# A hybrid decoder step: the down projection product by product over all of K, with the residual kept in SBUF

## The chip, the cores and the metric

The kernel runs on one core of one Trainium2 chip. The metric is the device time of one execution in microseconds. The kernel before took 2302.09 us (median of 3 runs, 2299.87 to 2306.37). One further execution was recorded by the hardware profiler; all profile lines of the kernel before come from it.

## The reference

One inference step of a decoder with a single layer, on 1040 prompt tokens (16 learned meta tokens and 1024 prompt tokens) and 8 sample tokens, 1048 tokens in all, in float32. The layer is a half-step feed-forward network (FFN), a mixer (HGRN2 heads and Mamba-2 heads) and a second half-step FFN:

```python
h = h + 0.5 * swiglu(rmsnorm(h, n1), w1g, w1u, w1d)
u = rmsnorm(h, nm) @ w_in            # then the HGRN2 and Mamba-2 groups
h = h + concat(hgrn_out, ssm_out) @ w_out
h = h + 0.5 * swiglu(rmsnorm(h, n2), w2g, w2u, w2d)
y = rmsnorm(h, norm_final)

def swiglu(x, wg, wu, wd):
    return (silu(x @ wg) * (x @ wu)) @ wd   # 1024 -> 2816 -> 1024
```

The change touches the last product of each `swiglu`, `(...) @ wd`, with the residual addition `h + 0.5 * (...)`, and what follows directly on it: the norm that feeds the mixer, and the final norm.

## The kernel before

**Layout.** Activations lie transposed: channels on the 128 partitions, the 1048 tokens along the free dimension. Tokens are cut into quarters of Q = 262; a half `c` has two quarters.

**Precision.** `Core.split` makes of a float32 tensor a rounded part (a cast on ScalarE, L137) and a remainder (a subtraction on VectorE, L138). `mm3` then issues three matmuls, high x high, high x low and low x high (L143 to L145).

**Seven products.** Each matrix product is done with one level of Strassen's scheme: a 2 x 2 block product with seven block products, numbered 1 to 7, in the Winograd form. The left operands are sums of weight blocks, the right operands sums of activation blocks. In the FFN a product's right operand has 262 columns for each of two halves.

**Gate/up phase.** `pair` does one block of 128 hidden channels of gate and up: 7 products x 2 halves x 4 blocks of K x 3 matmuls. There are 22 pairs, and each two of them make one hidden pair `i` (0 to 10). `left` loads four weight blocks (L320), forms four sums (L325) and seven splits; `Hidden.jobs` forms the seven right operands of the down phase for that hidden pair (subtractions at L503), splits each and stores the split halves to DRAM (tiles `hd`, L510).

**Down phase.** `down` takes the hidden pairs in three groups of 3, 4 and 4 (`Hidden.GROUPS`). For each group, and in it for each of four pairs of output tiles `j`, it runs all seven products and adds the partial result to the residual. So `Hidden.load` reads the split operands of a whole group at the group's start (L532, 28 transfers), `load_h` and `store_h` read and write the residual tiles for each group (L552, L559), and `left` reads the weights of a (group, j) once and forms all seven left operands. The posts (L570 to L580) combine the PSUM results: product 1 goes to a temporary on ScalarE (L573), 6 adds to it (L575), 2 closes the common part (L579, L580), the others are added with L570.

**Order.** Within the FFN the order on TensorE, VectorE, ScalarE and SP is written out by hand. A `Steps` object holds one step for each (product, half); other work is hung in front of a step by number (`S.before`), so a lead of 10 means ten steps ahead. Every engine works through its own queue in that order. All FFN transfers are issued by SP, one behind the other; an issue that waits holds all behind it.

**Buffers.** Tiles of 1056 columns come in 30 "u" slots and 8 "s" slots; weight buffers are 6 split (`ws`) and 8 raw (`r`); PSUM has two pairs of banks (`acc`) and four single banks (`mis`).

**Behind the phase.** `after1` squares and sums the residual for the next norm (`Norm.add`, ScalarE L201 and POOL L202), finishes the norm (`Norm.end`, a matmul with ones at L209), and forms the mixer's input (`plain_x`, L225 to L228). `after3` runs nine `final` blocks of 128 tokens each: transposes (L1365), squares (L1366), the scaling (L1372) and the store of the output.

Of the kernel before, what the change touches and what calls it, by code (L numbers as in the profile page):

```python
# [181 lines left out]
class Norm:  # L182
# [10 lines left out]
    def add(self, k, q):  # L193
        K = self.K
        hs = self.h[k][:, q * Q : q * Q + Q]
        if k == 0:
            self.sq[q] = K.t(Q)
            self.an = K.nc.scalar.activation(self.sq[q], hs, AF.Square)
        else:
            t = K.t(Q)  # L200
            self.an = K.nc.scalar.activation(t, hs, AF.Square)  # L201
            K.nc.gpsimd.tensor_add(self.sq[q], self.sq[q], t)  # L202

    def end(self, q, table=True):
        K = self.K
        if q % 2 == 0:
# [104 lines left out]
def left(K, S, s0, srcs, n, at, spare=None):  # L311

# [14 lines left out]
    def split(i, p):  # L327
        w[p] = K.split_w(raw[p], spare() if spare and i == 6 else None)
# [8 lines left out]
    splits = [lambda i=i, p=p: split(i, p) for i, p in enumerate(ORDER)]  # L337
# [11 lines left out]
def product(K, ps, w, op, n, first, last):  # L349
    for k in range(n):  # L350
        ks = slice(k * Q, k * Q + Q)
        wh, wl = (w[:, o + k * P : o + k * P + P] for o in (0, 512))
        K.mm3(ps, wh, wl, op[0][:, ks], op[1][:, ks], first and k == 0, last and k == n - 1, not first)


class Unit:
# [17 lines left out]
    def step(self, S, p, c, cs, mis=False):  # L374
        def mm():
            new = p in (1, 6, 5, 7)
            b = self.bank(p, cs, mis)
            product(self.K, b[:, cs.index(c)], self.w[p], self.ops[c][p], self.n, new, True)
# [87 lines left out]

class Hidden:

    GROUPS = (3, 4, 4)

    def __init__(self, K):
        self.K = K
        self.d = {}
        for g, n in enumerate(self.GROUPS):
            for p in ORDER:
                self.d[g, p] = K.dram.tile([P, 4, n, Q], F32, name=K.uid("hd"))
        self.of = [(g, i) for g, n in enumerate(self.GROUPS) for i in range(n)]
        self.n = 0  # L480

    def jobs(self, S, i, hid, e0, e1):

        K = self.K
        nc = K.nc
        g, j = self.of[i]
        t, b = {}, {}
        last = i == len(self.of) - 1
# [8 lines left out]
        def sub(p, x, y):  # L497
# [5 lines left out]
            nc.vector.tensor_sub(b[p], val(x), val(y))  # L503

        def split(p, w):
            self.n += 1
            st = K.slot("s" if last or self.n % 5 in (0, 2, 4) else "u", T, F32R)
            hi, lo = st[:, : 2 * Q], st[:, 2 * Q :]
            K.split(val(p), hi, lo)
            S.before(w, lambda: nc.sync.dma_start(self.d[g, p][:, :, j, :], st.bitcast(F32).rearrange("p (a t) -> p a t", a=4)))  # L510

        def at(i, fn, *args):
            S.before(i, lambda: fn(*args))

        at(e0 + 1, sub, 5, 12, 1)
        for k, p in ((3, 1), (5, 5)):
            at(e0 + k, split, p, e0 + k + 2)
        ks = range(1, 9) if last else range(1, 17, 2)
        for k, (fn, *args) in zip(ks, ((sub, 6, 3, 5), (split, 2), (sub, 7, 3, 12), (split, 3), (split, 6), (sub, 4, 2, 6), (split, 7), (split, 4))):
            at(e1 + k, fn, *args, *((e1 + k + 2,) if fn is split else ()))  # L520

    def load(self, S, g, s0, lead, tags):

        K = self.K
        n = self.GROUPS[g]
        ops = [{}, {}]

        def get(p, c, tag):
            ops[c][p] = []
            for part in range(2):  # L530
                t = K.slot(tag, n * Q, F32R)
                K.nc.sync.dma_start(t.bitcast(F32), self.d[g, p][:, 2 * part + c].rearrange("p n t -> p (n t)"))  # L532
                ops[c][p].append(t)

        for i, (p, c) in enumerate((p, c) for p in ORDER for c in range(2)):
            S.before(s0 + i - min(lead, 13 + i if tags[i] == "u" else 99), lambda p=p, c=c, i=i: get(p, c, tags[i]))
        return ops


def down(K, S, wdv, n, f0, j, ops, src, dst=None, h=None, then=None):  # L540

# [1021 lines left out]
```

## Time and profile before

| | |
|---|---|
| median of 3 runs | 2302.09 us |
| lowest, highest | 2299.87, 2306.37 us |
| the profiled execution | 2297.2 us |
| its span, first to last instruction | 2295.5 us |
| mean granted TensorE clock | 0.952 |
| busy: TensorE, VectorE, ScalarE, POOL | 2040.8, 1456.7, 799.2, 137.1 us |
| bytes moved by DMA | 353.11 MB |

How to read the lines that follow. PE is TensorE, PEld its weight loads, DVE VectorE, ACT ScalarE, SP the engine that issues the transfers. In a row of slices each digit is a fortieth of the span (57.4 us) and gives a busy share in tenths; PEclk is the clock granted to TensorE in tenths of full speed. A row of stretches gives, for each engine, the busy time and the number of instructions, and then the granted clock, the DMA engines' busy share and what they moved in GB/s (a share can slightly exceed 1). A wait row gives who waited for what, in total us, how many times, and the longest. A timeline row gives start and duration in us, engine, source line, operation and shape, and in brackets the idle time before it and what ended it. A row of one source line gives durations in ns (least, median, greatest), then first and last start in us.

### The profile page before, as it was taken

How to read it: one execution, taken by the hardware profiler on the slowest of the kernel's cores; microseconds unless marked ns; L12 is line 12 of the kernel's file. 1: busy time of each engine (PE TensorE's matmuls, PEld its weight loads, DVE VectorE, ACT ScalarE, POOL GpSimd, SP SyncE). 2: the span in 40 equal slices, each digit the busy share in tenths (PEclk: the TensorE clock that was granted, in tenths of full speed). 3: DMA queues.
4: the chain of work that ended last, by engine and by line, in shares of the span. 5: the costliest groups of instructions: out<-in, count | busy, mean ns of one | idle time of the engine just before them, and what ended most of it. 6: DMA issues, size and time to landing. Idle time of an engine off the chain costs nothing.

```text
span 2295.5 us, 38684 instructions
## 1 busy us (share of the span) xinstructions
PE 2040.8 (89%) x15550; PEld 1982.3 (86%) x15550; DVE 1456.7 (63%) x2516; ACT 799.2 (35%) x1511; POOL 137.1 (6%) x175
## 2 busy tenths in 40 slices
PE   3899999997787979979999999969999999778796
PEld 3799999997787869868989988869999999778795
DVE  5677777765454666577455456876777767554465
ACT  5433333332111353463432344433333333212122
POOL 1000000000000210131011101200000000000000
PEclk8999999998899989989999999989999999889897
DMA  3445445469869421163022153214454545986931
GB/s 114 122 131 160 140 132 158 136 183 322 316 242 345 143 82 35 60 178 87 30 66 75 34 170 124 90 38 131 144 151 136 162 128 167 352 288 233 353 122 75
DMA packets 344315, 353.11 MB, mean 154 GB/s; under 512 B 19584, under 2 KB 301440, under 8 KB 344128
## 3 DMA queue, kind: packets, MB, share of 16 engines
q1 hardware_dynamic: 343320, 348.49, 46.8%
q8 instruction: 123, 2.02, 0.4%
q10 hardware_dynamic: 592, 2.10, 0.3%
q14 instruction: 56, 0.46, 0.1%
q0 software_dynamic: 224, 0.04, 0.0%
HBM read 226.68 MB, written 123.95 MB: 153 GB/s over the span
## 4 chain that ended last, share of the span: by engine, by line
PE 45%; DVE 5%; DMA 4%; ACT 1%; issue 1%; SPq 0%; POOL 0%; DVEq 0%; ACTq 0%; POOLq 0%
PE acc L143 14%; PE acc L144 13%; PE acc L145 13%; DMA r<-in_w_ffn_down_dram 2%; PE mis L1234 2%; DMA u<-hd 1%; DVE r L325 0%; DVE u L1372 0%; PE mis L1273 0%; DVE s L1351 0%; DVE u L138 0%; DVE ws L138 0%; DVE u L253 0%; PE mis L1291 0%; PE mis L1329 0%
## 5 line engine op out<-in xcount | busy, mean ns | idle before, releaser
L143 PE MATMUL acc<-u,ws 128*128 128x262 f32 (+2 forms) x4512 | 1335.8, 297 | 162.1 <-ACT ws L137 74.2
L144 PE MATMUL acc<-u,ws 128*128 128x262 f32 (+2 forms) x4512 | 1324.6, 294 | 13.8 <-DVE u L138 10.7
L145 PE MATMUL acc<-u,ws 128*128 128x262 f32 (+2 forms) x4512 | 1322.1, 294 | 0.0
L143 PEld LDWEIGHTS acc<-u,ws 128*128 128x128 f32 x4512 | 866.1, 192 | 182.9 <-ACT ws L137 78.7
L144 PEld LDWEIGHTS acc<-u,ws 128*128 128x128 f32 x4512 | 870.9, 193 | 16.3 <-DVE u L138 12.2
L145 PEld LDWEIGHTS acc<-u,ws 128*128 128x128 f32 x4512 | 866.2, 192 | 0.4
L138 DVE TENSOR_TENSOR ws<-r,ws 128x512 fp32r<-128x512 f32 (+1 forms) x562 | 380.2, 680 | 252.7 <-ACT ws L137 251.7
L137 ACT CAST ws<-r 128x512 fp32r<-128x512 f32 (+1 forms) x562 | 325.4, 606 | 337.2 <-DMA r<-in_w_ffn_down_dram 126.7
L325 DVE TENSOR_TENSOR r<-r,r 128x512 f32<-128x512 f32 (+1 forms) x272 | 181.1, 679 | 126.8 <-DMA r<-in_w_ffn_down_dram 108.1
L421 ACT ACTIVATE t<-t 128x524 f32<-128x524 f32 (+1 forms) x46 | 28.7, 623 | 320.9 <-DVE t L420 320.9
L570 DVE SCALAR_TENSOR_TENSOR s<-acc,s 128x524 f32<-128x524 f32 (+1 forms) x120 | 78.6, 655 | 87.0 <-PE acc L145 86.1
L202 POOL TENSOR_TENSOR t<-t,t 128x262 f32<-128x262 f32 x56 | 48.5, 877 | 889.6 <-ACT t L201 888.9
L414 ACT ACTIVATE t<-acc 128x524 f32<-128x524 f32 (+1 forms) x46 | 27.1, 589 | 150.1 <-PE acc L145 150.1
L573 ACT ACTIVATE t<-acc 128x524 f32<-128x524 f32 (+1 forms) x26 | 14.9, 573 | 175.6 <-PE acc L145 175.6
L410 ACT COPY t<-acc 128x524 f32<-128x524 f32 (+1 forms) x46 | 26.6, 578 | 134.9 <-PE acc L145 134.9
L138 DVE TENSOR_TENSOR s<-s,s 128x524 fp32r<-128x524 f32 x98 | 68.4, 698 | 0.4 <-ACT s L137 0.4
L137 ACT CAST s<-s 128x524 fp32r<-128x524 f32 x98 | 61.7, 630 | 8.9 <-DVE s L503 8.9
L428 DVE TENSOR_TENSOR s<-t,t 128x524 f32<-128x524 f32 (+1 forms) x92 | 58.5, 677 | 1.6
L138 DVE TENSOR_TENSOR u<-u,u 128x1048 fp32r<-128x1048 f32 x32 | 41.5, 1311 | 26.7 <-ACT u L137 26.7
L420 DVE TENSOR_TENSOR t<-acc,t 128x524 f32<-128x524 f32 (+1 forms) x46 | 31.2, 679 | 33.9 <-PE acc L145 31.3
L1234 PEld LDWEIGHTS mis<-s,u 128*128 128x128 f32 x320 | 39.1, 198 | 9.2 <-issue 9.0
L1234 PE MATMUL mis<-s,u 128*128 128x64 f32 x320 | 40.3, 280 | 7.2 <-DVE u L1246 7.1
(355 smaller groups left out, 1718.4 us busy)
## 6 DMA issues: line engine op xcount, KB each, us to landing
hd<-s SPq DMA_DIRECT2D x126, 524.0 KB
u<-hd SPq DMA_DIRECT2D x106, 524.0 KB
hd<-u SPq DMA_DIRECT2D x60, 524.0 KB
s<-hd SPq DMA_DIRECT2D x46, 524.0 KB
r<-in_w_ffn_gate_dram SPq DMA_DIRECT2D x88, 256.0 KB
r<-in_w_ffn_up_dram SPq DMA_DIRECT2D x88, 256.0 KB
u<-hd SPq DMA_DIRECT2D x56, 393.0 KB
r<-in_w_ffn_down_dram SPq DMA_DIRECT2D x64, 256.0 KB
```

The source lines that it names most:

```text
L137: self.nc.scalar.copy(hi, src)
L138: self.nc.vector.tensor_sub(lo, src, hi.bitcast(F32))
L143: mm(ps, whi, xhi, start=first, stop=False, skip_group_check=more)
L144: mm(ps, whi, xlo, start=False, stop=False, skip_group_check=more)
L145: mm(ps, wlo, xhi, start=False, stop=last, skip_group_check=more)
L202: K.nc.gpsimd.tensor_add(self.sq[q], self.sq[q], t)
L325: nc.vector.tensor_tensor(raw[p], raw[x], raw[y], op)
L420: nc.vector.tensor_add(temp("g1", cs), b, temp("v", cs))
L421: nc.scalar.activation(temp("g1", cs), temp("g1", cs), AF.Silu)
L428: nc.vector.tensor_mul(halves(hid[0][:, n * 2 * Q : n * 2 * Q + 2 * Q])[:, cs], temp(f"g{n}", cs), temp(f"u{n}", cs))
L570: nc.vector.scalar_tensor_tensor(t, b, 0.5, t, ALU.mult, ALU.add)
L1234: nc.tensor.matmul(ps[:, 64 * c : 64 * c + 64], kg[:, P * c : P * (c + 1)], qv[:, c, :, 1], start=True, stop=True)
```

## The change

The down phase is reordered. The outer loop is now over the seven products in the order 1, 5, 6, 7, 3, 4, 2 (`DORDER`); within one product it goes over the four pairs of output tiles `j`, and for each over all 11 hidden pairs, in three parts of 4, 4 and 3 (`GROUPS`) that accumulate in one PSUM pair.

- `Hidden.jobs` no longer splits the right operands; it stores them unsplit, one transfer each of half the bytes.
- `Hidden.load` loads one product's operands in six transfers (part, half) and splits them in SBUF, spread over 24 steps: loads from 22 steps and splits from 16 steps ahead of the product.
- The eight residual tiles are loaded once into the eight "s" slots and stay there; every product adds its result directly to each of the residual quarters that it belongs to (one to four updates on VectorE); the temporaries on ScalarE are gone.
- Weight blocks are loaded for each (product, j, part): 9 blocks for each (j, part) instead of 4, since the blocks are no longer kept between products. The running sum of products 5, 6 and 3 is kept in six "u" slots. A block is loaded 13 steps, summed 8 steps and split 7 steps ahead of its use.
- In the last product the halves are the outer loop, so the first half of the tokens is complete after 12 of its 24 steps. Quarters 1 and 3 are complete before it.
- `after1` ends the norms of quarters 1 and 3 in product 4 and forms the mixer's input of the first half during the last product. `after3` runs final blocks 3, 7 and 8 during product 4, blocks 0, 1 and 2 during the second half of product 2, and 4, 5 and 6 behind it.

```diff
+FP = DFF // P // 2
+DORDER = (1, 5, 6, 7, 3, 4, 2)
+GROUPS = [(0, 4), (4, 4), (8, 3)]
 class Hidden:
-    GROUPS = (3, 4, 4)
...
+        self.d = {p: K.dram.tile([P, 2, FP, Q], F32, name=K.uid("hd")) for p in ORDER}
...
-        def split(p, w):
-            st = K.slot("s" if last or self.n % 5 in (0, 2, 4) else "u", T, F32R)
-            hi, lo = st[:, : 2 * Q], st[:, 2 * Q :]
-            K.split(val(p), hi, lo)
-            S.before(w, lambda: nc.sync.dma_start(self.d[g, p][:, :, j, :], ...))
+        def store(p):
+            K.nc.sync.dma_start(self.d[p][:, :, i, :], halves(val(p)))
...
+    def load(self, S, p, at):
+        def load(g, c):
+            i, n = GROUPS[g]
+            op[c][g] = K.slot("u", n * Q, F32R), K.slot("u", n * Q, F32R)
+            K.nc.sync.dma_start(op[c][g][1].bitcast(F32), self.d[p][:, c, i : i + n].rearrange("p n t -> p (n t)"))
+        def split(g, c):
+            hi, lo = op[c][g]
+            K.split(lo.bitcast(F32), hi, lo)
...
+def down(K, S, wdv, hidden, src, h, after):
+    for o in range(KT):
+        S.before(s0 + (-4, 2, 8, 9)[o // 2], lambda o=o: load_h(o))
+    def pieces(p, j, g, b, tag):
...
+        for a in {1: (11,), 5: (21, 22), 6: (11,), 7: (11, 21), 3: (12,), 4: (22,), 2: (12,)}[p]:
+            S.before(b - 13, lambda a=a: load(a))
+        if p in (5, 6, 7, 3):
+            x, y = {5: (21, 22), 6: (0, 11), 7: (11, 21), 3: (12, 0)}[p]
+            S.before(b - 8, lambda: sum_(x, y, ALU.add if p == 5 else ALU.subtract))
+        S.before(b - 7, split)
+    def matmuls(p, j, g, c, op, ps):
+        product(K, ps, w[p, j, g], op[c][g], GROUPS[g][1], g == 0, g == 2)
+    def post(p, j, cs, b):
+        for i, n in {1: ((0, 0), (0, 1), (1, 0), (1, 1)), 5: ((0, 1), (1, 1)), 6: ((0, 1), (1, 0), (1, 1)), 7: ((1, 0), (1, 1)), 3: ((0, 1),), 4: ((1, 0),), 2: ((0, 0),)}[p]:
+            t = hs[2 * j + i][:, cs, n]
+            nc.vector.scalar_tensor_tensor(t, b, 0.5, t, ALU.mult, ALU.add)
...
+    for a, p in enumerate(DORDER):
+        b = s0 + 24 * a
+        if a == 0:
+            at = [b + k for k in (-14, -11, -11, -9, -9, -7)], [b + k for k in (-8, -7, -6, -5, -4, -2)]
+        else:
+            at = [b - 22 + 3 * m for m in range(6)], [b - 16 + 3 * m for m in range(6)]
+        op = hidden.load(S, p, at)
...
+        for q in (1, 3):
+            S.before(e3 + q + 1, lambda q=q: nm.end(q))
+        S.before(e0, lambda: new_x(K))
...
+        for i, at in ((3, e3 + 6), (7, e3 + 11), (8, e3 + 16), (0, e0 + 2), (1, e0 + 5), (2, e0 + 8), (4, e1), (5, e1), (6, e1)):
+            S.before(at, lambda i=i: final(K, a, o, h, nf[0], K.slot("u", D), i))
```

202 lines of the change are left out of this document (85 added, 117 removed).

## The prediction

> **What bounds the kernel now.** I read the slices of the page first, then busy time by stretch, then the waits inside the slow stretches, then single instructions.
>
> ```profile
> span 2295.5 us, 38684 instructions
> ...
> PE   3899999997787979979999999969999999778796
> ...
> PEclk8999999998899989989999999989999999889897
> DMA  3445445469869421163022153214454545986931
> ```
>
> TensorE is the bound in most slices. The digits fall in two places (slices 10 to 13 and 35 to 38) where the DMA digits rise to 8 and 9: the two down phases.
>
> ```profile
> core 0: us, PE busy (x) PEld busy (x) DVE busy (x) ACT busy (x) POOL busy (x), PEclk, DMA share, GB/s
> 120.00:500.00 380.00, 380.00 (x3127) 380.00 (x3126) 279.45 (x440) 135.28 (x250) 0.00 (x0) 1.00 0.47 144
> 506.30:834.70 328.40, 258.98 (x1999) 255.37 (x1998) 179.12 (x291) 79.15 (x162) 20.34 (x27) 0.91 0.75 261
> 517.00:524.00 7.00, 0.91 (x8) 0.69 (x6) 1.78 (x4) 0.51 (x1) 0.00 (x0) 0.80 1.08 363
> 542.50:552.50 10.00, 0.42 (x4) 0.21 (x3) 2.91 (x7) 2.13 (x5) 0.00 (x0) 0.63 1.08 355
> 603.00:618.00 15.00, 0.14 (x2) 0.00 (x0) 2.02 (x4) 1.14 (x2) 0.00 (x0) 0.62 1.05 377
> ...
> 1946.20:2275.30 329.10, 263.81 (x2026) 260.25 (x2026) 171.85 (x295) 65.46 (x132) 0.00 (x0) 0.90 0.70 246
> ```
>
> In the gate/up phase TensorE is busy all the time at clock 1.00. In the down phase it stops for 7, 10 and 15 us with every DMA engine full, and comes back at a clock of about 0.6.
>
> ```profile
> ACT ws L137 <- DMA r<-in_w_ffn_down_dram: 63.3, 8, 14.9
> DVE r L325 <- DMA r<-in_w_ffn_down_dram: 53.9, 6, 14.1
> ...
> PEld acc L143 <- ACT ws L137: 38.1, 5, 15.2
> ```
>
> The chain (waits of 506.3 to 834.7): TensorE waits for a split weight, ScalarE and VectorE wait for the raw weight, and that lies behind the group's operands in the DMA queue.
>
> **How much the stalls cost.** First and last start of the first product's post (L410) in each gate/up phase, and the last post of the first down phase:
>
> ```profile
> L410 ACT COPY t<-acc x20: 596/598/600, 118.2 to 506.3; 128x524 f32<-128x524 f32 x20
> L410 ACT COPY t<-acc x21: 596/597/599, 1537.3 to 1946.2; 128x524 f32<-128x524 f32 x21
> L570 DVE SCALAR_TENSOR_TENSOR s<-acc,s x5: 423/424/432, 821.6 to 834.7; 128x262 f32<-128x262 f32 x5
> ```
>
> A pair takes (506.3 - 118.2) / 19 = 20.43 us for 7 products x 2 halves x 4 blocks x 3 = 168 matmuls: 0.1216 us each, without a stall. Behind 506.3 stand 144 matmuls of the last pair and 4 x 7 x 11 x 2 x 3 = 1848 of the down phase: 242.2 us, so it could end at 748.5. It ends at 834.7: **86.2 us lost**. In the second FFN 1946.2 + 242.2 = 2188.4 against 2275.3 (end of the stretch above): **86.9 us lost**.
>
> **The change part by part.** Both kernels issue the same 1848 matmuls per FFN; all else is cover or collision.
>
> *Bytes of one down phase*, from shapes. Operands: 11 x 28 transfers of 128 x 262 floats = 41.3 MB before; unsplit half, 20.7 MB. Residual: 24 loads and 16 stores of 0.537 MB = 21.5 MB before; 8 loads, 4.3 MB. Weights: 48 loads, 11.5 MB before; 9 blocks per (j, group) instead of 4, so 108 loads, 26.0 MB. Together 74 MB before, 51 MB after: over 1848 x 0.1216 = 224.7 us that is 228 GB/s, against 355 to 377 at a full share above. So the mean no longer saturates.
>
> *Gate/up phase.* 77 splits (ACT and DVE) and half the store bytes leave. Cover: TensorE at 380 of 380 us; VectorE has 279. Gain 0, and no loss, since only work goes.
>
> *Entry of the down phase.* In the last 14 steps (14 x 12 x 0.1216 = 20.4 us) come product 1's operands (2.95 MB), six weight blocks (1.45 MB), two stores and two residual tiles (1.07 MB each). At the loads' 377 / 1.05 = 359 GB/s and the weights' and stores' 144 / 0.47 = 306 GB/s: 8.2 + 4.7 + 3.5 + 3.0 = 19.4 us. That just fits, in a burst, and SP takes its loads in order behind slots that TensorE frees. Bounds 0 and 7 us (the stall at 517); I take 3, as the sum fits.
>
> *VectorE in the down phase.* It now splits weights, sums weights, splits the next product's operands and updates the residual in one queue.
>
> ```profile
> 502.38 0.69 DVE L138 TENSOR_TENSOR ws<-r,ws 128x512 fp32r<-128x512 f32 x1 [1.22 <-ACT ws L137]
> 502.99 0.70 DVE L138 TENSOR_TENSOR s<-s,s 128x524 fp32r<-128x524 f32 x1
> ...
> 538.23 0.55 DVE L138 TENSOR_TENSOR ws<-r,ws 128x384 fp32r<-128x384 f32 x1
> 538.70 0.70 DVE L138 TENSOR_TENSOR s<-s,s 128x524 fp32r<-128x524 f32 x1
> 539.31 0.70 DVE L570 SCALAR_TENSOR_TENSOR u<-acc,u 128x524 f32<-128x524 f32 x1
> 540.04 0.70 DVE L579 TENSOR_TENSOR u<-u,t 128x524 f32<-128x524 f32 x1
> 540.66 1.25 DVE L580 TENSOR_TENSOR u<-u,t 128x1048 f32<-128x1048 f32 x1
> 541.83 0.70 DVE L503 TENSOR_TENSOR s<-s,s 128x524 f32<-128x524 f32 x1
> ```
>
> Starts lie closer than durations: 0.61 us for 512 and 524 columns, 0.47 for 384, 1.17 for 1048, 0.73 where an update waits for the one ahead. For 786 columns I estimate 0.89, between 524 and 1048.
>
> ```profile
> 629.26 0.69 DVE L138 TENSOR_TENSOR ws<-r,ws 128x512 fp32r<-128x512 f32 x1 [2.77 <-ACT ws L137]
> ...
> 720.23 1.42 DVE L325 TENSOR_TENSOR r<-r,r 128x512 f32<-128x512 f32 x2 [11.97 <-DMA r<-in_w_ffn_down_dram]
> ```
>
> ```profile
> 628.61 2.17 ACT L137 CAST ws<-r 128x512 fp32r<-128x512 f32 x4
> ...
> 721.75 1.14 ACT L137 CAST ws<-r 128x512 fp32r<-128x512 f32 x2 [5.35 <-DVE r L325]
> ```
>
> A new wait: in products 5, 6, 7 and 3 a weight's split stands right behind its sum. Sum end to cast start is 0.10 us (721.65 to 721.75), the cast 0.62, its end to the subtraction 0.03: 0.75 us in which VectorE idles unless an operand split stands between. In the changed order that is so for 4 of 12; 8 are bare.
>
> Product 6, the heaviest, has 12 sums and 12 weight splits (8 x 0.61 + 4 x 0.47 = 6.8 each), 6 operand splits (4 x 1.17 + 2 x 0.89 = 6.5), 12 updates (8 x 0.61 + 4 x 0.73 = 7.8), 8 waits (6.6 with the lost overlap of 0.09) and some 0.6 behind two operand casts: 35.1 us. TensorE needs 264 x 0.1216 = 32.1. Products 5 and 7 come to 32.2 and 32.7, product 1 to 28, product 4 to 18. So VectorE falls 3.0 + 0.7 us behind. Splits are issued 7 steps ahead, and a PSUM pair must be read within 6 steps (6 x 11 x 0.1216 = 8.0 us, less the updates' 1.5): 6.5 us of cover. Cost 0 where it starts in time; without the cover up to 4 us.
>
> *DMA in products 5 and 7* (two blocks per piece): 5.77 MB / 306 + 2.95 MB / 359 = 18.9 + 8.2 = 27.1 us of 32.1. Product 5 follows four residual loads (2.15 MB, 6.0 us), so its first weights are late by some 3 us, which adds to the lag: 3.7 + 3, about the cover. Bounds for the whole middle 0 and 15 us per FFN (the longest wait for a weight above is 14.9); nearest is the sum, so I take 3. SP issues 24 weight loads in such a product, at 0.46 us 11 us of 32; an operand load that waits for its slot holds the weight loads behind it, and so the sums.
>
> ```profile
> L320 SPq DMA_DIRECT2D r<-in_w_ffn_down_dram x48: 367/457/3324, 509.1 to 779.6; - x48
> ```
>
> *Tails.* In the first FFN two norm matmuls wait for POOL in product 4 (about 2 us). Behind the last post TensorE now idles thus:
>
> ```profile
> 835.97 0.32 PE L143 MATMUL acc<-u,ws 128*128 128x350 f32 x1
> ...
> 843.41 0.66 PE L144 MATMUL acc<-u,ws 128*128 128x350 f32 x1 [3.15 <-DVE u L228]
> ```
>
> The changed order finishes the first half's normalized columns before the last post, so of 7.4 us I keep 2.4: gain 5 (bounds 0 and 7.4). In the second FFN five `final` blocks stand behind the last post; now three.
>
> ```profile
> 2278.98 1.41 DVE L1372 SCALAR_TENSOR_TENSOR u<-mis,ssq,u 128x512 f32<-128x512 f32 x2
> 2281.95 1.41 DVE L1372 SCALAR_TENSOR_TENSOR u<-mis,ssq,u 128x512 f32<-128x512 f32 x2
> ...
> ```
>
> ```profile
> 2252.79 1.04 PE L1365 MATMUL mis<-ident,s 128*128 128x128 f32 x8
> ```
>
> Each is 2.97 us: gain 5.9. The six moved in between cost TensorE 6 x 1.04 = 6.2 and, by estimate, 3 for waits in VectorE's queue (bounds 0 and 10).
>
> **The sum**, against the profiled execution (2297.2 us, span 2295.5 plus 1.7; 0.2% under the median of 2302.1, so I carry the difference over to the median). First FFN: 86.2 - 3 - 3 - 2 + 5 = 83.2. Second: 86.9 - 3 - 3 - 6.2 - 3 + 5.9 = 77.6. Together 160.8: 2136.4 for the profiled execution, **2141 us** for the median. With no stall at all it is 17 less (2124); with all upper bounds (2 x 4 + 2 x 12 + 7 + 5 = 44 more) 2185.
>
> **A rule against it.** The Trainium skill, page "VectorE: DVE Perf Modes", section "The DRAIN you can't avoid", says that after every operation the next does not start until the pipeline is empty, and that chaining does not avoid it. By that rule full durations count, and the lag would outgrow the cover; that is part of the next paragraph. This trace disagrees: starts 0.61 us apart at durations of 0.70.
>
> **The rivals.**
> *VectorE becomes the bound.* With full durations (0.69, 0.55, 1.31, 0.70) product 6 takes 37.8 us, products 5 and 7 some 35.0: a lag of 11.5, of which 6.5 are covered, so 5 per FFN: 2151. The section named gives this time. If each bare wait is twice as long, as in gate/up:
>
> ```profile
> DVE ws L138 <- ACT ws L137: 71.7, 48, 2.1
> ```
>
> (1.5 us each), 24 waits add 18 us per FFN: 2141 + 2 x (3.7 + 18 - 6.5) = 2171. For it: VectorE's sum is at the limit. Against: in gate/up other work of ScalarE stood in between.
>
> *Weights still late.*
>
> ```profile
> 2046.02 7.86 DMA r<-in_w_ffn_down_dram
> ...
> 2073.31 10.04 DMA r<-in_w_ffn_down_dram
> ```
>
> Eight raw buffers hold four pieces of products 5 and 7. At 8 us to land plus 2 for sum and split a piece comes each 2.5 us, TensorE takes one each 2.7; at 10 us it is 3.0, or 4 us per product: 2141 + 16 = 2157. At the longest wait (14.9) it is 4.2, or 18 per product: 2213. Against: these rows are from a saturated queue.
>
> *Slower: the next product's operands don't load ahead.* If the 30 "u" slots, which two sets of 12 and 6 sums fill exactly, come free only at the product's end, each of 14 products waits for 2.95 MB / 359 = 8.2 us, a cast and a subtraction (2), and restarts at a clock near 0.62: some 11.5 us, and 14 x 11.5 = 161 us takes the whole gain; at 12.5 us it ends at 2316. Against: the loads reuse slots whose product ended two steps earlier.
>
> **How the numbers follow.** Forecast 0.63 (2124 to 2160), VectorE-bound 0.17 (2151 to 2185), weights late 0.15 (2157 to 2213), operands not ahead 0.05. Range 2122 to 2190, which leaves out most of the late weights and the slower case. 0.3% is 7 us, what a measurement can tell: faster 0.95, same 0.01, slower 0.04.
>
> **What would show it.** In the changed profile: the stalls of 7 to 15 us gone, clock 1.00 through the down phases, a share of DMA near 0.7 there; the first down phase ending near 757, VectorE busiest in product 6, waits of ACT's weight casts on DMA near zero. It is wrong if TensorE's waits for split weights stay at tens of us (see whether DMA or VectorE released them), or if gaps recur every 32 us, at the products' starts.

## The result and the profile after

The changed kernel takes 2182.86 us (median of 4 runs, 2178.09 to 2183.97), the kernel before 2303.42 us beside it (median of 4): a ratio of 0.9473, 95% interval 0.9453 to 0.9493. The forecast was 2141 us. Against the profiled executions (2297.2 us before, 2182.6 us after) the gain is 114.6 us where 160.8 were forecast: 46 us are missing.

From the page of the changed kernel, the span and the slices for TensorE, its clock and the DMA engines:

```profile
span 2180.8 us, 38344 instructions
...
PE   3899999999998989889999998969999999999996
...
PEclk8999999999999899989999999989999999999998
DMA  3433333337967421262022053312332333587851
```

The two holes of slices 10 to 13 and 35 to 38 are nearly closed. Small ones are left. Busy time by stretch, one stretch for each product of the first down phase in its order 1, 5, 6, 7, 3, 4, 2 (columns as in the prediction):

```profile
526.40:564.40 38.00, 34.03 (x266) 33.65 (x265) 24.45 (x35) 10.00 (x15) 0.00 (x0) 0.96 0.92 283
564.40:598.10 33.70, 32.34 (x265) 32.17 (x266) 27.40 (x41) 12.41 (x18) 0.00 (x0) 1.00 0.92 274
598.10:631.70 33.60, 32.51 (x266) 32.13 (x264) 27.27 (x42) 12.40 (x18) 0.00 (x0) 1.00 0.59 173
631.70:665.30 33.60, 32.69 (x264) 32.35 (x265) 26.79 (x40) 12.41 (x18) 0.00 (x0) 1.00 0.87 261
665.30:697.50 32.20, 32.20 (x266) 32.20 (x265) 24.59 (x34) 14.96 (x27) 5.13 (x6) 1.00 0.61 185
697.50:740.30 42.80, 35.60 (x271) 35.13 (x271) 24.37 (x33) 23.26 (x43) 10.88 (x12) 0.88 0.49 146
740.30:788.70 48.40, 40.09 (x280) 38.72 (x279) 28.05 (x58) 19.64 (x42) 8.15 (x12) 0.89 0.51 156
```

A product without a stall takes 264 x 0.1216 = 32.1 us. Product 3 does. Products 5, 6 and 7 are 1.5 us over, product 1 is 6 over, product 4 10.6 and product 2 over 15, at a clock of 0.88 to 0.89. So what is missing stands at the two ends of the phase, not in its heavy middle.

The first and last start of the first product's post in the two gate/up phases (L409 now), and of the posts (L582) in the last part of each down phase:

```profile
L409 ACT COPY t<-acc x20: 596/596/599, 119.4 to 507.6; 128x524 f32<-128x524 f32 x20
...
L409 ACT COPY t<-acc x23: 378/598/598, 1439.0 to 1896.0; 128x524 f32<-128x524 f32 x21, 128x262 f32<-128x262 f32 x2
...
L582 DVE SCALAR_TENSOR_TENSOR s<-acc,s x13: 418/431/705, 703.8 to 788.3; 128x262 f32<-128x262 f32 x8, 128x524 f32<-128x524 f32 x5
...
L582 DVE SCALAR_TENSOR_TENSOR s<-acc,s x35: 420/697/705, 1999.5 to 2166.0; 128x524 f32<-128x524 f32 x27, 128x262 f32<-128x262 f32 x8
```

By the prediction's own measure the first phase could end 242.2 us behind 507.6, at 749.8, and ends at 788.3: 38.5 us lost (forecast 8). The second could end at 2138.2 and ends at 2166.0: 27.8 lost (forecast 15.2). Those two differences are 43 of the 46 missing us.

Two of the stalls, on TensorE's timeline (start, duration, operation; in brackets the idle time before it and what ended it):

```profile
700.36 0.28 PE L145 MATMUL acc<-u,ws 128*128 128x262 f32 x1
707.84 1.24 PE L209 MATMUL mis<-t,ones 128*128 128x262 f32 x2 [7.20 <-POOL t L202]
...
744.18 0.28 PE L145 MATMUL acc<-u,ws 128*128 128x262 f32 x1
748.16 0.56 PE L143 MATMUL acc<-u,ws 128*128 128x262 f32 x1 [3.70 <-DVE s L582]
748.51 0.42 PE L144 MATMUL acc<-u,ws 128*128 128x262 f32 x1
```

and the post on VectorE that ended the second:

```profile
747.59 0.42 DVE L582 SCALAR_TENSOR_TENSOR s<-acc,s 128x262 f32<-128x262 f32 x1
```

In product 4 the norm's matmul (L209) stands in TensorE's order before POOL has summed its squares. In product 2, TensorE is about to begin the second box, and waits for the post of the *first* box. `K.psum` hands out the two halves of one PSUM pair in turn, and such a wait stands ahead of the second box of a pair: 3.98, 0.89, 2.66 and 1.86 us in the first phase, 1.99, 0.90, 3.56 and 3.60 in the second (from start to start).

The waits of the whole first down phase (total us, times, longest):

```profile
DVE ws L138 <- ACT ws L137: 43.7, 45, 2.5
...
PE acc L143 <- DVE s L582: 14.0, 10, 3.7
...
ACT u L137 <- DMA u<-hd: 10.9, 4, 6.0
```

TensorE no longer waits for ScalarE's splits. What it waits for, beside the 7.2 us for POOL, is VectorE's posts, and VectorE itself waits 43.7 us for ScalarE's casts.

### The profile page after: what moved, and what is told of

Same layout as the page of the kernel before. It is cut to its first block, busy times and chain, and to the rows that moved or that the text cites. A ratio compares the mean times of both kernels' runs of the same rounds, so it can differ in the third digit from the quotient of the medians.

```text
span 2180.8 us, 38344 instructions
## 1 busy us (share of the span) xinstructions
PE 2029.1 (93%) x15550; PEld 1972.1 (90%) x15550; DVE 1395.1 (64%) x2358; ACT 786.8 (36%) x1415; POOL 137.6 (6%) x175
## 4 chain that ended last, share of the span: by engine, by line
PE 72%; DVE 13%; DMA 5%; ACT 4%; issue 3%; POOL 1%; SPq 1%; ACTq 0%; DVEq 0%; POOLq 0%
PE acc L143 22%; PE acc L144 21%; PE acc L145 21%; DVE u L138 2%; DVE s L582 2%; DMA u<-hd 2%; DVE ws L138 2%; PE mis L1248 2%; ACT ws L137 2%; DMA r<-in_w_ffn_down_dram 1%; DVE u L563 1%; ACT u L137 1%; DVE u L261 1%; DVE r L563 1%; PE mis L1287 0%
## 5 line engine op out<-in xcount | busy, mean ns | idle before, releaser
L144 PE MATMUL acc<-u,ws 128*128 128x262 f32 (+2 forms) x4504 | 1319.1, 293 | 10.6 <-DVE u L138 10.6
L143 PEld LDWEIGHTS acc<-u,ws 128*128 128x128 f32 x4504 | 860.3, 191 | 81.0 <-issue 28.1
L144 PEld LDWEIGHTS acc<-u,ws 128*128 128x128 f32 x4504 | 863.7, 192 | 13.5 <-DVE u L138 12.1
L138 DVE TENSOR_TENSOR ws<-r,ws 128x512 fp32r<-128x512 f32 (+1 forms) x480 | 328.1, 688 | 259.3 <-ACT ws L137 259.3
L137 ACT CAST ws<-r 128x512 fp32r<-128x512 f32 (+1 forms) x480 | 274.8, 611 | 163.4 <-PE acc L145 80.0
L138 DVE TENSOR_TENSOR u<-u,u 128x1048 fp32r<-128x1048 f32 (+1 forms) x116 | 139.2, 1206 | 44.5 <-ACT u L137 44.0
L324 DVE TENSOR_TENSOR r<-r,r 128x512 f32<-128x512 f32 x176 | 118.6, 692 | 15.5 <-DMA r<-in_w_ffn_up_dram 14.0
L137 ACT CAST u<-u 128x1048 fp32r<-128x1048 f32 (+1 forms) x116 | 116.1, 1013 | 26.5 <-DMA u<-hd 21.5
L582 DVE SCALAR_TENSOR_TENSOR s<-acc,s 128x524 f32<-128x524 f32 (+1 forms) x120 | 77.5, 662 | 36.7 <-PE acc L145 35.6
L137 ACT CAST ws<-u 128x512 fp32r<-128x512 f32 (+1 forms) x72 | 42.1, 585 | 121.7 <-DVE u L563 113.7
L409 ACT COPY t<-acc 128x524 f32<-128x524 f32 (+1 forms) x46 | 26.6, 579 | 156.9 <-PE acc L145 156.9
L138 DVE TENSOR_TENSOR ws<-u,ws 128x512 fp32r<-128x512 f32 (+1 forms) x72 | 47.0, 653 | 36.8 <-ACT ws L137 36.8
L419 DVE TENSOR_TENSOR t<-acc,t 128x524 f32<-128x524 f32 (+1 forms) x46 | 31.2, 679 | 59.9 <-PE acc L145 59.9
L411 DVE TENSOR_TENSOR t<-acc,t 128x524 f32<-128x524 f32 (+1 forms) x46 | 31.3, 680 | 36.0 <-PE acc L145 36.0
```

The source lines that it names most:

```text
L137: self.nc.scalar.copy(hi, src)
L138: self.nc.vector.tensor_sub(lo, src, hi.bitcast(F32))
L143: mm(ps, whi, xhi, start=first, stop=False, skip_group_check=more)
L144: mm(ps, whi, xlo, start=False, stop=False, skip_group_check=more)
L324: nc.vector.tensor_tensor(raw[p], raw[x], raw[y], op)
L411: nc.vector.tensor_add(temp("v", cs), b, temp("z", cs))
```

## The experiments

Twelve kernels ran. Each time is a median with its ratio to the kernel before on the same chip (the changed kernel's is 0.9473). The duration of each product, first phase / second phase, worked out from the first matmul of a product to the first of the next in the one profiled execution of each kernel, in us:

| run | 1 | 5 | 6 | 7 | 3 | 4 | 2 |
|---|---|---|---|---|---|---|---|
| changed kernel | 38.0/36.8 | 33.7/33.8 | 33.7/33.8 | 33.6/33.6 | 32.2/32.2 | 42.7/34.8 | 47.6/46.1 |
| e1_psum | 38.6/38.1 | 33.7/33.8 | 33.6/33.5 | 33.6/33.6 | 32.2/32.1 | 42.4/34.8 | **34.0/34.8** |
| e2_norm | 39.4/37.0 | 33.7/33.7 | 33.6/33.8 | 33.6/33.6 | 32.2/32.2 | **33.0**/34.8 | 49.1/49.0 |
| e3_sum | 40.4/39.1 | 35.0/33.7 | **32.1/32.2** | **32.1/32.1** | 32.2/32.3 | **34.5**/34.8 | 45.1/48.7 |
| e4_resid | **35.2/34.3** | 33.7/36.1 | 33.7/32.2 | 33.6/33.4 | 32.2/32.2 | 42.5/34.8 | 47.5/48.8 |
| e6_all | 35.4/34.7 | 33.9/34.2 | 32.2/32.3 | 32.1/32.1 | 32.2/32.2 | 32.9/34.8 | 34.0/34.8 |
| e5_late | 34.2/35.4 | 37.7/38.3 | 32.5/32.2 | 35.5/36.4 | 33.2/32.3 | 34.9/34.8 | 52.0/56.1 |
| e7_bytes | 38.6/37.0 | 33.7/33.7 | 33.6/33.9 | 33.6/33.6 | 32.2/32.2 | 42.0/34.8 | 46.6/53.2 |
| e10_rush | 38.6/37.0 | 62.5/63.6 | 34.0/34.7 | 62.2/61.2 | 33.7/34.5 | 41.4/34.8 | 47.6/47.5 |
| e12_rush5 | 45.6/44.4 | 42.1/41.5 | 35.1/34.9 | 41.8/42.9 | 34.6/33.7 | 40.1/34.8 | 46.5/48.9 |
| e11_rushact | 37.3/37.4 | 53.5/57.5 | 39.4/37.8 | 55.1/54.7 | 36.3/36.4 | 42.9/34.8 | 47.8/47.8 |
| e8_dve | 39.5/38.1 | 40.9/40.9 | 41.9/42.1 | 40.1/40.2 | 32.4/32.4 | 42.5/34.8 | 47.5/48.9 |

Products 4 and 2 of the second phase hold 2.4 us of the final blocks' transposes each. Product 2 of the second phase varies by some 3 us (46.1 to 49.0) between kernels that leave it alone, and more in e7_bytes (53.2); smaller differences there say nothing.

### Where the missing 46 us are

**e1_psum.**

```diff
-                                box.append(K.psum()[:, :Q])
+                                box.append(K.psum2()[:, 0, :Q])
```

> Only the PSUM places of product 2, the last of each down phase, are changed: every box of 128 x 262 gets a PSUM pair of its own, of which it uses one half, where in the changed kernel two boxes that follow each other share a pair. Theory (the second half of a pair waits for the post that reads its first half): the gaps ahead of the second box of each pair go (3.98, 0.89, 2.66 and 1.86 us in the first phase, 1.99, 0.90, 3.56 and 3.60 us in the second), with most of the slow clock behind them, and the time falls from 2182.9 to between 2160 and 2170 us. Rival (VectorE is simply late in product 2, and whoever needs it waits): the gaps move to the next box that needs the same pair, and the time stays between 2178 and 2185 us.

2164.3 us, ratio 0.9375 (0.9347 to 0.9403). Product 2 of the first phase, by stretch:

```profile
740.30:774.30 34.00, 32.77 (x268) 32.48 (x266) 22.35 (x45) 17.16 (x36) 7.00 (x11) 1.00 0.71 207
```

Product 2 falls by 13.6 and 11.3 us to what it needs, and the clock is 1.00. VectorE is busy for a larger share of it (22.4 of 34.0 us, against 28.1 of 48.4 above). So it was not VectorE's speed: a box that could have gone to a free bank waited because its neighbour's bank was still to be read. The theory held; this is the largest single miss.

Not all of it reaches the time in this execution. By the table the two phases are 23.8 us shorter, the span only 11.5 (2169.3 against 2180.8), because the stretch between the phases takes 11.6 us longer (1120.6 against 1109.0 from the last matmul of the first phase to the last L409). The phase's last post now starts at 779.6, 5 us after that last matmul, so some of VectorE's work stands behind product 2; whether that is the cause is not shown.

**e2_norm.**

```diff
-            S.before(e3 + q + 1, lambda q=q: nm.end(q))
+            S.before(e3 + 2 * q + 8, lambda q=q: nm.end(q))
```

> Only the two norm matmuls of the first down phase that stand in product 4 are changed: they stand at 10 and 14 steps into the stretch from product 4's start in place of 2 and 4. Theory (TensorE's 7.5 us gap in product 4 is this one matmul standing in its order before its squares are summed): the gap and the 1.6 us of slow clock in that product go, nothing takes their place, the second down phase stays as it is, and the time falls by 7 to 10 us to between 2173 and 2176 us. Rival (VectorE's lag is what stands behind it, and TensorE that no longer waits there runs into VectorE at the next box): a gap of the same size comes in product 4 or product 2, and the time stays between 2180 and 2185 us.

2176.5 us, 0.9427 (0.9406 to 0.9448). Product 4 of the first phase falls from 42.7 to 33.0 us, and product 2 gives back 1.5. The stall did not move to another place as a whole. The time fell by 6.4 us, a little less than the 7 to 10 of the theory.

**e3_sum.**

```diff
-            S.before(b - 8, lambda: sum_(x, y, ...))
+            S.before(b - 10, lambda: sum_(x, y, ...))
```

> Only the place of the down weights' sums in the order is changed: ten steps ahead of their use in place of eight, so that on VectorE a split of the group ahead stands between a sum and the split that needs ScalarE's cast of that sum. Theory (VectorE's lag in products 5 to 7 is the round trip over ScalarE, and what is late in products 4 and 2 is this lag carried on): VectorE's waits for ScalarE's weight casts, 48.4 us in the first phase, fall below 20 us, the gap of 2.3 us in product 6 goes in both phases, the norm matmul's gap of 7.5 us falls to 4 us or less, product 2's gaps fall by a third or more, and the time falls to between 2166 and 2175 us. Rival (VectorE's own work, 35.1 us in product 6 against 32.1 us of TensorE, is the limit whatever the order): the waits go but product 6 keeps its gap, and the time stays between 2179 and 2185 us.

2171.3 us, 0.9404 (0.9374 to 0.9433). VectorE's wait for ScalarE's weight casts, same view as above:

```profile
DVE ws L138 <- ACT ws L137: 18.7, 12, 2.5
```

43.7 us became 18.7, products 6 and 7 run without a loss, and TensorE's wait for the norm's squares in product 4 shrinks from 7.2 to 1.2 us though the norm's matmul was not moved. So the squares were late because the posts ahead of them were, and these because VectorE carried its lag of products 5 to 7 on. But product 2 gained only 2.5 us in the first phase and none in the second, which the expectation had wrong (e1 shows why). Product 1 lost 2.3 us in each phase, and product 5 another 1.3 in the first: over these two products the sums' wait for a weight's DMA rose from 2.0 to 5.5 us, as they now ask earlier for weights that are still under way.

**e4_resid.**

```diff
-        S.before(s0 + (-4, 2, 8, 9)[o // 2], lambda o=o: load_h(o))
+        S.before(s0 + (-4, 2, 10, 16)[o // 2], lambda o=o: load_h(o))
```

> Only the loads of the residual's last four tiles are changed: they stand 10 and 16 steps into the down phase in place of 8 and 9. Theory (the loss in product 1, 8.7 us in the first phase and 7.4 in the second, comes from DMA that is asked for everything at once: the share is 1.08 between 540 and 560 us): product 1's loss falls by a half in each phase, and the time falls by 5 to 8 us to between 2175 and 2178 us. Rival (product 5's operands and the weights alone fill the queue, or the lag comes from the hidden blocks' stores): the time stays between 2180 and 2185 us.

2178.0 us, 0.9434 (0.9406 to 0.9462). Product 1 falls by 2.8 and 2.5 us: about half its loss, as expected. In the second phase product 5 takes 2.3 us more and product 6 1.6 less. The time itself is not clear of noise: its interval and the changed kernel's (0.9453 to 0.9493) overlap. The other half of product 1's loss stays. Product 5's operands are the likely rest: e5_late, which issues them in the last nine steps of product 1 in place of all through it, brings it to 34.2 and 35.4 us, but product 5 then pays 4.0 and 4.5. So what fills this other half is not shown.

**e6_all.** All four edits, with product 5's sums left at eight steps.

> The four edits together: a PSUM pair of its own for each box of product 2, the two norm matmuls at 10 and 14 steps, the sums of products 6, 7 and 3 ten steps ahead (product 5's stay at eight, since in the run with all of them moved product 1 lost 2.3 us more), and the last residual loads at 10 and 16 steps. Theory (the four losses are separate, so what each edit saved in its own run adds up): product 2 gives 13.6 and 11.3 us, product 4 of the first phase 8 to 9.7, products 5 to 7 six times 1.5, product 1 2.8 and 2.5, in sum 47 to 49 us, and the time is 2134 to 2140 us. Rival (they are one lag of VectorE seen at several places, so the gains overlap, as the norm gap fell to 1.7 us by the earlier sums alone): no more than 35 us in all, 2148 to 2160 us.

2141.3 us (2136.77 to 2149.27), 0.9277 (0.9254 to 0.9299). The seven products by stretch, in the first phase:

```profile
525.70:561.10 35.40, 32.54 (x266) 32.14 (x264) 24.25 (x35) 9.88 (x15) 0.00 (x0) 1.00 0.89 277
561.10:595.00 33.90, 32.58 (x264) 32.22 (x265) 27.59 (x42) 13.79 (x20) 0.00 (x0) 1.00 1.01 302
595.00:627.20 32.20, 32.18 (x265) 32.20 (x265) 31.78 (x49) 14.92 (x22) 0.00 (x0) 1.00 0.70 215
627.20:659.30 32.10, 32.10 (x266) 32.10 (x265) 26.11 (x39) 12.42 (x18) 0.00 (x0) 1.00 0.92 273
659.30:691.50 32.20, 32.20 (x266) 32.20 (x266) 23.00 (x30) 15.03 (x29) 9.94 (x10) 1.00 0.57 178
691.50:724.50 33.00, 33.00 (x271) 32.87 (x270) 20.13 (x28) 19.02 (x34) 6.60 (x8) 1.00 0.48 146
724.50:758.50 34.00, 32.77 (x268) 32.47 (x266) 22.89 (x46) 17.17 (x36) 7.02 (x11) 1.00 0.73 222
```

The clock is 1.00 throughout, and the phases are 28.8 and 16.0 us shorter (sums of the table's rows), 44.8 against 47 to 49 forecast. Product 2 gives 24.9, product 4 9.8 and product 1 4.7, all near what the expectation put for them. Products 5 to 7 give 5.4 in place of 9, because product 5, whose sums were left, did not gain. So the losses are separate, as the theory had it, though the time is 1.3 us above its range: 41.3 of the 44.8 us reach the span. This version beats both kernels; its ratio is 0.0196 below the changed kernel's. That it comes out at the 2141 us of the forecast is in part chance, for the terms do not match one by one.

### What the gain is made of

**e5_late.**

```diff
-            at = [b - 22 + 3 * m for m in range(6)], [b - 16 + 3 * m for m in range(6)]
+            at = [b + k for k in (-9, -9, -7, -7, -5, -5)], [b + k for k in (-3, -2, -1, 0, 1, 2)]
```

> One part of the change is undone: the hidden operands of products 5, 6, 7, 3, 4 and 2 are loaded 9 to 5 steps ahead of the product's start in place of 22 to 7, and split 3 steps ahead to 2 steps into it, in the place of 16 to 1 ahead. Bytes and instructions stay as they are. Theory (the overlap of one product's operands with the product ahead is what removed the stalls): 2.95 MB come in a rush beside the weights, at the 283 GB/s of product 1 over 10.4 us alone, weights stand behind them in the queue, and each of the twelve products loses 4 to 9 us, so the time is 2230 to 2290 us. Rival (fewer bytes are what removed the stalls, and the order of the loads matters little): 2180 to 2195 us.

2191.7 us, 0.9484 (0.9467 to 0.9501): the rival. Products 5 and 7 lose 2 to 5 us, product 2 loses 4 and 10, and products 1 and 4 gain, product 4 of the first phase 7.8. The long lead of the operand loads is worth under 10 us of the gain on balance (8.8 in the medians, and the two intervals overlap); the losses of the single products are larger and partly made up by the gains.

**e7_bytes.**

```diff
         op = hidden.load(S, p, at)
+        if 0 < a < 6:
+            for o in range(KT):
+                S.before(b + 3 * o, lambda o=o: nc.sync.dma_start(K.dram.tile([P, T], F32, name=K.uid("cp")), src(o)))
```

> The other part of the change is undone as to its bytes: in products 5, 6, 7, 3 and 4 the eight source tiles of 0.54 MB are each copied once from DRAM to DRAM on SP's queue, one in every three steps, 8.6 MB read and written in a product, 43 MB in a phase, where the kernel before moved 88 MB more than the changed one over both phases. The order of all other work stays. Theory (the bytes were the bound): 8.6 MB at 280 GB/s are 31 us more for DMA in products that already keep it at 0.59 to 0.92 of 33 us, so each of these products takes 50 to 60 us and the time is 2340 to 2420 us, above the kernel before. Rival (with the loads a product ahead there is room to wait for them, and the copies lie beside the matmuls): below 2220 us.

2184.5 us, 0.946 (0.9427 to 0.9492): no cost. Products 5, 6, 7 and 3 of its first phase, by stretch:

```profile
563.40:597.10 33.70, 33.70 (x265) 33.70 (x266) 27.41 (x41) 12.40 (x18) 0.00 (x0) 0.95 1.00 334
597.10:630.70 33.60, 32.49 (x266) 32.13 (x265) 27.27 (x42) 12.42 (x18) 0.00 (x0) 1.00 1.01 349
630.70:664.30 33.60, 32.69 (x265) 32.33 (x266) 26.79 (x40) 12.47 (x18) 0.00 (x0) 1.00 0.98 330
664.30:696.50 32.20, 32.20 (x266) 32.20 (x265) 24.55 (x34) 15.01 (x27) 5.13 (x6) 1.00 1.05 387
```

A copy moves its 0.54 MB once, so 40 of them add 21.5 MB to a phase's 51, about the 74 MB of the kernel before (the expectation counted them twice). All DMA engines are busy all the time, as in the stalls before, and the products take just as long as without the copies. So the number of bytes is not what made the kernel faster, as long as they are spread and nothing waits for them, and a full DMA share is not by itself a stall.

**e10_rush.** The same 40 copies, in two rushes.

```diff
+        if p in (6, 3):
+            for o in range(20):
+                S.before(b - 13, lambda o=o: nc.sync.dma_start(K.dram.tile([P, T], F32, name=K.uid("cp")), src(o % KT)))
```

> The same 40 copies from DRAM to DRAM in each down phase as in the run with the bytes back, which cost nothing there (2184.5 us), but in two rushes of 20, each issued at one place: 13 steps ahead of product 6 and of product 3, just ahead of that product's first weights. Instructions and bytes are the same as in that run. Theory (not the bytes but a rush that stands in SP's queue ahead of the weights stops TensorE): 20 x 0.537 = 10.7 MB at the 387 GB/s seen there take 28 us, the weights behind them are due on TensorE 13 steps (17 us) after their issue, so TensorE stops for about 11 us at each of four rushes and comes back at a slow clock: 2225 to 2250 us, with gaps near 11 us that waits put down to the weights' DMA. Rival (transfers that are under way at once share the engines, and the weights come through beside the copies): 2180 to 2197 us.

2301.6 us (median of 10 runs), 0.9983 (0.9964 to 1.0003). The whole gain is gone, by the order of the transfers alone. (That the time comes out just at the old one is chance: it follows from the size of the rush that was chosen.) The timelines of SP, VectorE and TensorE around the first rush:

```profile
582.96 26.18 SPq L597 DMA_DIRECT2D cp<-xT  x20
610.33 1.72 SPq L553 DMA_DIRECT2D r<-in_w_ffn_down_dram  x2
...
593.38 0.55 DVE L138 TENSOR_TENSOR ws<-u,ws 128x384 fp32r<-128x384 f32 x1
623.10 0.69 DVE L563 TENSOR_TENSOR u<-u,r 128x512 f32<-128x512 f32 x1 [29.17 <-DMA r<-in_w_ffn_down_dram]
...
626.92 0.56 PE L143 MATMUL acc<-u,ws 128*128 128x262 f32 x1 [28.66 <-DVE s L582]
```

The mechanism is the theory's, and worse than it sized: 29 us at each rush, not 11. SP needs 26 us to issue 20 copies, the first weight behind them lands 40 us after the first copy's issue, VectorE stands in its order at that weight's sum, and behind the sum wait the posts of the product that is *running*. TensorE needs their PSUM pairs, so it stops 15 us after the rush begins (626.92 - 28.66 = 598.3).

Why SP needs 26 us is in its own waits, from 582 to 640 us:

```profile
SPq L597 <- DMA cp<-xT: 13.5, 12, 1.5
```

In this trace each transfer signals its landing on one of eight semaphores, which are used in turn, and an issue waits for the landing of the transfer eight places ahead of it. So no more than eight are under way, 12 of the 20 copies wait for one of the first 12, and the first weight is not even issued until the thirteenth copy has landed.

The Trainium skill, page "DMA: Bandwidth & Descriptors", section "Two DMAs through the same engine are not ordered", says that within one queue of one engine descriptors start in order. No run here shows when a descriptor starts; the trace shows that the weights, issued at 610.33 behind the last copies, land at 623.1, 13 us later.

**e9_half.** In the kernel before, half the rush; the low parts are left out:

```diff
-            for part in range(2):
-                t = K.slot(tag, n * Q, F32R)
-                K.nc.sync.dma_start(t.bitcast(F32), self.d[g, p][:, 2 * part + c].rearrange("p n t -> p (n t)"))
-                ops[c][p].append(t)
+            t = K.slot(tag, n * Q, F32R)
+            K.nc.sync.dma_start(t.bitcast(F32), self.d[g, p][:, c].rearrange("p n t -> p (n t)"))
+            ops[c][p] = [t, t]
```

> The kernel before with half the rush: the low parts of the hidden operands are not loaded, and the product of the weights' high part with the operands' low part uses the high part a second time, so this part of the computation is left out. 14 transfers of a group in place of 28, the order of all else as before. Theory (what the kernel before loses is the group's rush of 28 transfers, 15 MB and 42 us at 359 GB/s, ahead of weights that are due sooner): with 7.5 MB and 21 us the stalls of 86.2 and 86.9 us fall to a third or less, and the time to 2170 to 2215 us. Rival (what it loses lies elsewhere, in the residual's round trips or in weights loaded by (group, j)): above 2260 us.

2208.4 us, 0.9565 (0.9519 to 0.961). The wait of TensorE's weight loads for split weights in the first down phase, 38.1 us before:

```profile
PEld acc L143 <- ACT ws L137: 10.6, 5, 5.0
```

With 14 transfers at a group's start in place of 28, more than half of the loss goes, with grouping and residual traffic as they were: by the prediction's measure 86.2 and 86.9 us lost become 38.5 and 36.0 (last posts at 787.0 and 2187.8). That is less than the two thirds of the theory, and what makes the rest is not shown. The run also needs half as many slots and half the operand bytes, so it does not separate the queue from these. In the changed kernel e7 and e10 do: bytes that are spread cost nothing, and a rush that needs no slot is enough for such stalls.

**e12_rush5.** The copies in eight rushes of 5: for each of four products, one 13 steps and one a single step ahead of its start (so the second stands ahead of the weights for its middle).

```diff
+        if p in (5, 6, 7, 3):
+            for o in range(10):
+                S.before(b - 13 + 12 * (o // 5), lambda o=o: nc.sync.dma_start(K.dram.tile([P, T], F32, name=K.uid("cp")), src(o % KT)))
```

> The same 40 copies in each down phase once more, in eight rushes of 5: 13 steps ahead of products 5, 6, 7 and 3 and again in the middle of each. Theory (a rush costs what it outlasts the lead of the weights behind it): with 20 copies the first weight landed 40 us after the first copy's issue and TensorE stopped 15.3 us after it; 5 copies, 2.7 MB, need about 9 us at 300 GB/s and some 3 to land, so they stay within the 15.3 us and cost nothing or a few us: 2183 to 2200 us. Rival (each copy ahead of weights costs its own time, 118 us for 80 copies in the run with rushes of 20): 2270 to 2305 us.

2237.5 us, 0.9692 (0.966 to 0.9723): neither. Products 1, 5 and 7 lose 7 to 9 us each, products 6 and 3 one or two. A rush of 5 is nearly hidden where DMA has room (a share of 0.59 and 0.61 without copies) and costs 7 to 9 us a product where it is busy (0.87 to 0.92). The theory's flat lead of 15 us is too simple: the likely reason is that the lead is used up already where weights are late.

**e11_rushact.** The rushes of 20, issued by ScalarE (the edit against e10_rush).

```diff
-                S.before(b - 13, lambda o=o: nc.sync.dma_start(...cp...))
+                S.before(b - 13, lambda o=o: nc.scalar.dma_start(...cp...))
```

> The rushes of 20 copies as they were, but issued by ScalarE's queue in place of SP's; bytes, places and all other work the same. Theory (the order within SP's queue is what holds the weights back): the weights are issued in time and come through beside the copies, so VectorE's wait for a weight's DMA falls from 29 us to below 10, and what is left is ScalarE, whose casts stand behind 20 issues of 0.47 us: 2200 to 2240 us. Rival (the engines work through what was asked for first, whichever queue it came by, or ScalarE's issues are held up by the full queue as SP's were, 26 us for 20): TensorE still stops for 20 us or more at each rush: 2270 to 2305 us.

2288.8 us, 0.9914 (0.9881 to 0.9947): the rival's second half. On ScalarE's timeline:

```profile
584.94 23.96 ACTq L597 DMA_DIRECT2D cp<-xT  x19
609.02 0.62 ACT L137 CAST ws<-u 128x512 fp32r<-128x512 f32 x1 [23.12 <-DMA cp<-xT]
```

19 issues take 24 us, 1.26 us each, and the casts stand behind them. VectorE no longer waits for a weight's DMA. But SP was held too; its waits from 582 to 625 us:

```profile
SPq L517 <- DMA cp<-xT: 28.3, 2, 26.8
```

ScalarE's and SP's transfers take their turn on the same eight semaphores, so SP issues nothing from 583 to 610 us: its next issue waits for a copy. The theory's premise, weights issued in time, did not hold. Whether weights that are issued would pass a rush on another queue stays open.

**e8_dve.** VectorE given 12 more subtractions in products 5, 6 and 7:

```diff
             w[p, j, g] = K.split_w(v, t)
+            if p in (5, 6, 7):
+                n_ = v.shape[1]
+                nc.vector.tensor_sub(t[:, 512 : 512 + n_], v, t[:, :n_].bitcast(F32))
```

> VectorE is given more to do: in products 5, 6 and 7 the subtraction that makes the low part of each weight group is done twice, 12 more operations of 0.55 to 0.70 us in a product, 7.9 us. Theory (VectorE is at its limit there: 33.9 us of work and waits in product 6 against 32.1 us of TensorE): each of these products takes 38 to 42 us, and the time rises by 35 to 55 us to between 2218 and 2238 us. Rival (VectorE is busy 27.3 of the 33.6 us of product 6, and the rest is slack that more work can use): 2183 to 2198 us.

2228.2 us, 0.9649 (0.963 to 0.9668), as the theory said: 7.9 us more work costs 6.5 to 8.3 us a product. VectorE is at its limit there, though in product 6 of the changed kernel it is busy for only 27.3 of 33.6 us; the waits for casts, which stand in its order, fill the rest.

## Why the prediction was right and wrong

**Right.** The sign, the cause of the stalls before as far as e9 and e10 show it, and the middle of the phase. *VectorE in the down phase* and *DMA in products 5 and 7* were priced together at 3 us for each FFN and cost 4.7 and 4.9. The new wait was seen (0.75 us for each bare sum and split; 43.7 us over 45 waits is 0.97), the lag of some 3 us in product 6 mostly hides, and e3 removes what is left. In the rival *VectorE becomes the bound* product 6 takes 37.8 us; it takes 33.6, and 32.2 with the sums earlier. That rival went by the rule of the Trainium skill's page "VectorE: DVE Perf Modes", section "The DRAIN you can't avoid"; the same section adds that a next operation that is not held starts earlier, and the starts 0.61 us apart at durations of 0.70 are such a case. The rival *operands don't load ahead* did not occur, and e5 prices even late loads at 9 us on balance. The gate/up phase is unchanged: (507.6 - 119.4) / 19 = 20.43 us for a pair.

**In the range by luck.** The time lies outside the forecast's own band (2124 to 2160, chance 0.63) and inside those of two rivals, *VectorE becomes the bound* (2151 to 2185) and *weights still late* (2157 to 2213). Neither is what happened: product 6 stays far below 37.8 us, the waits for ScalarE's casts are 0.97 us each and not 1.5, and in the first phase VectorE and ScalarE wait 7.7 us in all for a weight's DMA. The range held because it left room for losses other than those that came.

Of the signs, ScalarE's weight casts wait 5.7 us for DMA in the first phase in place of 63.3, as said. The clock is 1.00 in the middle but 0.88 and 0.89 in products 4 and 2, the DMA share runs from 0.49 to 0.92, VectorE is as busy in product 5 as in product 6 (27.4 and 27.3 us), one stall of 7.2 us is left, and the first phase's last post starts at 788.3 and not near 757 (in e6 at 763.7).

**Wrong in emphasis.** The prediction sets 74 MB against 51 MB and says "the mean no longer saturates". e7 and e10 show that the mean is not what counts: with the old bytes back the time is the same, and with them back in rushes it is the old time.

**The steps that failed**, with the rest of the sum:

| term | forecast, 1st / 2nd FFN | measured |
|---|---|---|
| entry and product 1 | 3 / 3 | 7.2 / 6.0 |
| middle, products 5 to 7 | 3 / 3 | 4.7 / 4.9 |
| norm matmuls in product 4 | 2 / - | 9.7 |
| product 2, with the finals' waits | 0 / 3 | 15.3 / 11.6 |
| finals' work on TensorE | - / 6.2 | 4.8 |

(Measured: the product's duration less 32.1, without the other TensorE work in products 4 and 2, 0.9 and 0.2 us in the first FFN and 2.4 each in the second; the entry holds 1.3 us ahead of product 1.)

- *Product 2* had no term of its own in the first FFN, and the second had 3 us "by estimate". The sum counted the PSUM cover of a pair of banks, right for six products; it did not ask where the seventh takes its banks. e1 shows that the shared pair is the cause: 13.6 and 11.3 us.
- *The norm matmuls* were named, with the right wait, and priced at "about 2 us". The price missed that the post in front of the squares comes late: e3 cuts the wait of 7.2 us to 1.2 without touching the matmul, e2 removes it.
- *The entry* was priced 3 of a possible 7 "as the sum fits". That sum stopped at the phase's first step; the collision is in product 1 itself, for one half with the last residual tiles (e4), for the other likely with product 5's operands.

*Tails.* Behind the last post stand 2180.8 - 2166.0 = 14.8 us, 20.2 before: 5.4 of the 5.9 forecast. Between the phases, last post to last L409, 1107.7 us against 1111.5: 3.8 of 5, though this stretch ran from 1099.0 to 1115.3 us in e1 to e4, which change nothing in it, so neither number is a measurement. The first phase also starts 1.3 us later (507.6 against 506.3), and with that the 46 us are made up: 43.1 in the phases, 0.5 and 1.2 in the tails, 1.3 ahead.

## What to carry to other kernels

Ask of a full DMA queue not how many bytes it holds but what stands in it behind a rush: the same 40 copies of 0.54 MB in each phase cost nothing one at a time and some 117 us in rushes of 20 (e7, e10). Count how many transfers can be under way; here it was eight, whichever engine issued them (e11). Where engines work in order, follow a late transfer to the instruction that is stuck behind it; here a sum for the *next* product held up the posts of the running one. And a reordered loop has ends: price its first and last turns with their own buffers and neighbours, since two thirds of the missing time lay there, and a sixth in one matmul placed too early.

## What was not expected of the hardware

Issuing in a rush took long, but by waiting: SP needed 26.2 us for 20 copies (1.31 us each), while a copy's issue itself had a median of 0.47 us; 13.5 us of the rest stand in the row above as waits for earlier copies. ScalarE's 19 took 24.0 us.

VectorE's subtractions take longer while POOL adds. In e6_all, VectorE's rows and then POOL's:

```profile
673.19 0.54 DVE L138 TENSOR_TENSOR ws<-u,ws 128x384 fp32r<-128x384 f32 x1
...
680.99 1.11 DVE L138 TENSOR_TENSOR ws<-u,ws 128x384 fp32r<-128x384 f32 x1
...
677.31 4.37 POOL L202 TENSOR_TENSOR t<-t,t 128x262 f32<-128x262 f32 x4 [6.36 <-ACT t L201]
```

The same split takes 0.54 us alone and 1.11 beside POOL's four additions. The Trainium skill, page "SBUF — State Buffer", section "SBUF: two separate sides", says that a VectorE operation with two SBUF inputs and a GpSimd operation that reads SBUF lock each other out of a shared pair of ports. The direction agrees. It costs nothing in e6_all, where VectorE has slack in that product, product 3 (23.0 us busy of 32.2, TensorE without a stall).
